# Two-operand elementwise work of the token mixers, from GpSimd to VectorE, in a hybrid RWKV-7 and HGRN2 decoder step

## The chip, the cores and the metric

One NeuronCore of a Trainium2 chip runs the whole step as one program. The metric is the device time of one execution in microseconds. The engines are named as the profile names them: PE is TensorE, DVE is VectorE, ACT is ScalarE, POOL is GpSimd, and SP starts most of the transfers. Each engine works through its own queue in order.

## What is computed

One layer of a decoder with 1024 prompt tokens and 8 sample sequences of 4 tokens each, at a model width of 1024, all in fp32:

```python
h = rmsnorm(x, norm1) * (1 + sc1) + sh1                 # sh1, sc1, gt1, ... = silu(c) @ w_ada + b_ada
p = h @ w_in                                            # 1024 -> 3840
x_rw = p_rw + (p_prev - p_rw) * mu_shift                # token shift, RWKV part (1792 columns)
y_rw = rwkv7(x_rw, state_wkv)                           # 8 heads of 64
f = lb + (1 - lb) * sigmoid(f_raw)
y_hg = hgrn2(silu(q), 1 - f, log(f), i, state_hgrn)     # 4 heads of 128
x = x + gt1 * (concat([y_rw, y_hg]) @ w_out)
h = rmsnorm(x, norm2) * (1 + sc2) + sh2
x = x + gt2 * (square(relu(h @ w_up)) @ w_down)         # 1024 -> 4096 -> 1024
y = rmsnorm(x, norm_f)
```

The new shift row and the two recurrent states, of the prompt and of each sample sequence, are returned as well.

## The kernel before

**Stages.** The profiled execution falls into two parts. The mixers (0 to 935 us) hold the first norm, the input projection, both recurrences and the conditioning vectors `mod`. From 935 us on come the output projection and the MLP, where `L1086` splits weights and `L1097` multiplies; no line of the change is run there.

**Mixers.** Tokens go in four quarters of 256; the first carries the 32 sample tokens too, 288 columns. Activations are kept transposed, features on the partitions. Before the first quarter the start computes the norm of quarter 0 (`x0` times its reciprocal root, `rstd`), the first sixteen tiles of `w_ada` (`ada_block`, subtractions at L236) and the modulation (`modulate0`, L306 to L310, and the remainder `l` at L1064). The norms of the later quarters are computed beside the projection by `norms`, whose sums of squares are added at L264.

**Projection.** A matrix product is taken in three single-pass products: every fp32 operand is split into a rounded part `hi` and a remainder `lo`. `load_w` loads a 128-column tile of `w_in` in two halves of 128x512, rounds each half on ScalarE (L172) and subtracts it from the original (L176). `gemm` then issues hi x hi, hi x lo, lo x hi (L186 to L188). The first use of each of the thirty tiles subtracts; of these sixty halves `load_in` gives three in four to GpSimd:

```python
w = self.load_w(wp, io["w_in"][m], wlo_d.get(m), m in seen, (V, V) if m in seen else [(G, G), (G, V)][self.nw % 2])
```

For tiles 14 to 29 the remainder is written to DRAM and loaded again in later quarters; for tiles 0 to 13 VectorE subtracts each time. A projected RWKV tile is evicted by ScalarE (`praw`, L583 for the samples' `psmp`), VectorE forms the shifted difference (L585, L586 for the prompt, L590, L591 for the 32 sample columns), and GpSimd does the small copies around it (L574 to L592): it fills the first column of `praw` and of `psmp` before the eviction and takes the last column into `shift_sb` after it.

**RWKV.** The prompt goes in eight groups of 128 tokens, the samples in a ninth. `rwkv_prep` loads the shifted projections of a group (`X`), forms `kk` (L687), the scaled keys (L690, L691) and the bonus term: the product at L715, a matmul, the result at L720, four transfers of it into `bot`, and the addition of a bias to `bot` at L727. After that `rwkv_attn` masks the score blocks (L758). `rwkv_inv` inverts the diagonal blocks by substitution on GpSimd (L825, L827), one short instruction after the other. `rwkv_chain` and `rwkv_finish` follow; `rwkv_finish` scales the output rows (L1014) before they are transposed. The sample group masks its operands at L954 and L994.

**HGRN.** `hgrn_mix` works head by head on a quarter. Its product at L438 is transposed by TensorE (L401). `hgrn_sample` multiplies the sample states and their operands by masks (L537, L540, L542).

**Order.** Generators are interleaved by `mixers`; the tile framework then orders each engine's queue by its own estimate of the times, so code that changes engines lets the whole order of the mixers be laid out anew. Line numbers of the profile are those of the kernel before; in the changed kernel every line from 92 on has a number smaller by one.

Of the kernel before, what the change touches and what calls it, by code (L numbers as in the profile page):

```python
# [90 lines left out]
AB = 3  # L91
XM = (0, 1, 2, 3, 4, 5, 6, 7)
EPS = 1e-6
# [39 lines left out]
class Kernel:  # L133
# [256 lines left out]
    def hgrn_mix(self, hd, qi, pool, pp, t, y_out):  # L390
# [46 lines left out]
        V.tensor_tensor(qe, q, f, op=ALU.mult)  # L437
        G.tensor_tensor(r, k, r, op=ALU.mult)  # L438
        kt = pool.tile([P, NC_, P], F32, tag="hkt", name="hkt", bufs=MB)
# [43 lines left out]
    def hgrn_sample(self, h0, pool, pp, y_out):  # L483
# [43 lines left out]
        for j in range(2):  # L527
            el = f[:, cols[j]].rearrange("p (b t) -> p b t", t=TS)[:, :, TS - 1:TS]
            po = pp.tile([SC, P], F32, tag="h", name="ps_os")
            nc.tensor.matmul(po, lhsT=att[:, j, :], rhs=vt[:, j, :], start=True, stop=False)  # L530
            for g in range(2):
                gs = slice(g * 4, (g + 1) * 4)
                s0 = pool.tile([P, 4, P], F32, tag="hs0", name="hs0", bufs=B_hs0)
                nc.sync.dma_start(s0, io["hgrn_in"][h0 + j, :, gs, :])

                qs = pool.tile([P, 4, SC], F32, tag="hqs", name="hqs", bufs=B_hqs)
                G.tensor_tensor(qs, qe[:, cols[j]].unsqueeze(1).to_broadcast([P, 4, SC]), self.tokm[:, gs, :], op=ALU.mult)  # L537
                for b in range(4):
                    nc.tensor.matmul(po, lhsT=qs[:, b, :], rhs=s0[:, b, :], start=False, stop=g == 1 and b == 3)
                G.tensor_tensor(s0, s0, el[:, gs, :].to_broadcast([P, 4, P]), op=ALU.mult)  # L540
                vm = pool.tile([SC, 4, P], F32, tag="hvm", name="hvm", bufs=B_hvm)
                G.tensor_tensor(vm, vt[:, j, :].unsqueeze(1).to_broadcast([SC, 4, P]),  # L542
                                self.seqm[0:SC, gs].unsqueeze(2).to_broadcast([SC, 4, P]), op=ALU.mult)
                pd = pp.tile([P, 4, P], F32, tag="h", name="ps_ss")
                nc.tensor.matmul(pd, lhsT=kt[:, j, :], rhs=vm, start=True, stop=True)
                V.tensor_tensor(s0, s0, pd, op=ALU.add)
                nc.scalar.dma_start(io["hgrn_s"][h0 + j, :, gs, :], s0)
                yield
            nc.scalar.activation(o[:, j, :], po, AF.Copy)
            nc.scalar.activation(sq[:, j, :], o[:, j, :], AF.Square, accum_out=ss[:, j:j + 1])  # L550
# [79 lines left out]
    def rwkv_prep(self, g, pool, pp, x_d):  # L630
# [55 lines left out]
        kk = t4("kk")  # L686
        G.tensor_tensor(kk, k, bc4(self.vec("k_k")), op=ALU.mult)  # L687
        for j in range(4):
            V.tensor_scalar(cs[:, j, :], a[:, j, :], self.vec("k_a", j), self.omka[:, j:j + 1], op0=ALU.mult, op1=ALU.add)
        G.tensor_tensor(k, k, cs, op=ALU.mult)  # L690
        G.tensor_tensor(a, a, sg, op=ALU.mult)  # L691
        sq = cs
# [21 lines left out]

        G.tensor_tensor(cs, r, k, op=ALU.mult)  # L715
        bo = kk
# [7 lines left out]
        for h in range(2):  # L724
            for e in range(2):
                nc.sync.dma_start(btq[e * 64:(e + 1) * 64, :, h, :], boq[h * 64:(h + 1) * 64, :, e, :])
        G.tensor_tensor(bt, bt, bc4(self.vec("lnx_b")), op=ALU.add)  # L727

# [212 lines left out]
    def rwkv_chain_sample(self, g, pool, pp):  # L941
# [9 lines left out]
        def alone(y):  # L951
            ax = pool.tile([P, 4, NS, 32], F32, tag="iat", name="ax", bufs=B_iat)
            for j in range(4):
                G.tensor_tensor(ax[:, j], ar[:, j, 0, y, :32].unsqueeze(1).to_broadcast([P, NS, 32]), self.tokm, op=ALU.mult)  # L954
            return ax
# [33 lines left out]
        for j in range(4):  # L989
            ps = pp.tile([P, NS, 64], F32, tag=PT[2], name="ps_Ss")  # L990
            for h in range(2):
                hs = slice(h * 64, h * 64 + 64)
                rm = pool.tile([P, NS, 64], F32, tag="U", name="rm", bufs=B_U)
                G.tensor_tensor(rm, R[:, j, h, :].unsqueeze(1).to_broadcast([P, NS, 64]),  # L994
                                self.seqm.unsqueeze(2).to_broadcast([P, NS, 64]), op=ALU.mult)
                nc.tensor.matmul(ps[hs], lhsT=bt[:, j, hs], rhs=rm, start=True, stop=True)
# [6 lines left out]
    def rwkv_finish(self, g, pool, pp, y_d):  # L1003
# [8 lines left out]
        for c in range(nch):  # L1012
            oc = g["oc"][:, c]
            G.tensor_tensor(oc, oc, rs[:, c].unsqueeze(2).to_broadcast([P, 4, 64]), op=ALU.mult)  # L1014
            for q in range(2):
# [551 lines left out]
    def mixers(self, wp, x_d, y_d):  # L1567
# [3 lines left out]
        with (tc.tile_pool(name="h", bufs=1) as hp, tc.tile_pool(name="hg", bufs=1) as hg,  # L1571
# [17 lines left out]
            def norms():  # L1589

                for qi in (1, 2, 3):
# [3 lines left out]
                    for k in range(KT):  # L1595
                        with tc.issue_after(self.last_split.ins):
                            self.square_add(hp, x(k), acc, k == 0, nc.gpsimd)
                        if k % 2:
# [21 lines left out]
            with tc.tile_pool(name="ada", bufs=1) as ap:  # L1620
# [8 lines left out]
                for k in range(KT):  # L1629
                    (nc.gpsimd if k in XM else nc.vector).tensor_tensor(x0[:, k, :], x0[:, k, :], r0, op=ALU.mult)  # L1630
                for b in range(4):
# [15 lines left out]
            def load_in(m):  # L1647
                self.nw += 1
                V, G = nc.vector, nc.gpsimd
                w = self.load_w(wp, io["w_in"][m], wlo_d.get(m), m in seen, (V, V) if m in seen else [(G, G), (G, V)][self.nw % 2])  # L1650
                seen.add(m)
                return w
# [207 lines left out]
```

## Time and profile before

| | |
|---|---|
| median of 3 runs | 1751.42 us (1748.58 to 1761.52) |
| profiled execution | 1748.32 us, span of the instructions 1746.4 us |
| granted TensorE clock, mean | 0.95 of full |
| busy, share of the span | PE 92%, DVE 73%, ACT 52%, POOL 27% |
| POOL | 466.7 us busy, 977 instructions, all before 935 us |

A busy share is a mean over stages with different limits; the table by stage divides it up. A wait is put down to the engine or transfer that came last.

### The profile page before, as it was taken

How to read it: one execution, taken by the hardware profiler on the slowest of the kernel's cores; microseconds unless marked ns; L12 is line 12 of the kernel's file. 1: busy time of each engine (PE TensorE's matmuls, PEld its weight loads, DVE VectorE, ACT ScalarE, POOL GpSimd, SP SyncE). 2: the span in 40 equal slices, each digit the busy share in tenths (PEclk: the TensorE clock that was granted, in tenths of full speed). 3: DMA queues.
4: the chain of work that ended last, by engine and by line, in shares of the span. 5: the costliest groups of instructions: out<-in, count | busy, mean ns of one | idle time of the engine just before them, and what ended most of it. 6: DMA issues, size and time to landing. Idle time of an engine off the chain costs nothing.

```text
span 1746.4 us, 38086 instructions
## 1 busy us (share of the span) xinstructions
PE 1601.1 (92%) x14224; PEld 1491.0 (85%) x14224; DVE 1277.9 (73%) x2735; ACT 903.4 (52%) x1861; POOL 466.7 (27%) x977
## 2 busy tenths in 40 slices
PE   6787998999899999899988997999999999999895
PEld 3777887787788888788867997999999999999895
DVE  7777878786655657566776669655655869798998
ACT  6446543446466665657654446455444554443351
POOL 3755738546351625436340000000000000000000
PEclk9899889999889999998988998999999999999997
DMA  7676675866677775765547533443333442324122
GB/s 261 191 226 220 200 231 155 289 211 186 180 230 219 217 227 167 220 183 156 160 143 250 202 129 116 142 140 102 105 104 111 154 147 94 111 87 139 35 75 100
DMA packets 216168, 288.66 MB, mean 165 GB/s; under 512 B 48264, under 2 KB 119304, under 8 KB 212912
## 3 DMA queue, kind: packets, MB, share of 16 engines
q1 hardware_dynamic: 198112, 263.16, 47.7%
q10 hardware_dynamic: 17776, 23.01, 3.9%
q8 instruction: 112, 1.84, 0.4%
q14 instruction: 72, 0.59, 0.1%
q0 software_dynamic: 96, 0.07, 0.0%
HBM read 225.64 MB, written 58.29 MB: 163 GB/s over the span
## 4 chain that ended last, share of the span: by engine, by line
PE 60%; DVE 17%; DMA 8%; ACT 5%; issue 4%; POOL 4%; SPq 1%; ACTq 0%; DVEq 0%; POOLq 0%
PE ps_g L1097 36%; PE ps_in L186 3%; PE ps_in L187 3%; PE ps_in L188 3%; DMA wraw<-w_in 2%; POOL itmp L825 2%; POOL ixt L827 2%; PE ps_A L755 1%; PE ps_l L429 1%; DVE acc L1384 1%; DMA x<-xT 1%; DVE wlo L1086 1%; DVE bl L1380 1%; DVE wlo L176 1%; DMA iat<-at_d 1%
## 5 line engine op out<-in xcount | busy, mean ns | idle before, releaser
L1097 PE MATMUL ps_g<-bh,whi 128*128 128x264 f32 x1792 | 370.7, 287 | 13.6 <-ACT whi L1085 8.5
L1097 PE MATMUL ps_g<-bh,wlo 128*128 128x264 f32 x1792 | 369.9, 287 | 9.0 <-DVE wlo L1086 9.0
L1097 PE MATMUL ps_g<-bl,whi 128*128 128x264 f32 x1792 | 371.0, 287 | 1.4 <-DVE bl L1380 1.4
L186 PE MATMUL ps_in<-h,whi 128*128 128x256 f32 (+1 forms) x960 | 292.2, 306 | 17.8 <-ACT psmp L583 8.4
L1097 PEld LDWEIGHTS ps_g<-bh,whi 128*128 128x128 f32 x1792 | 282.6, 190 | 14.6 <-ACT whi L1085 8.7
L1097 PEld LDWEIGHTS ps_g<-bh,wlo 128*128 128x128 f32 x1792 | 281.1, 190 | 9.7 <-DVE wlo L1086 9.7
L187 PE MATMUL ps_in<-l,whi 128*128 128x256 f32 (+1 forms) x960 | 286.7, 299 | 3.0 <-DVE l L1064 2.1
L188 PE MATMUL ps_in<-h,wlo 128*128 128x256 f32 (+1 forms) x960 | 285.7, 299 | 3.8 <-DVE wlo L176 3.7
L1097 PEld LDWEIGHTS ps_g<-bl,whi 128*128 128x128 f32 x1792 | 281.9, 190 | 1.6 <-DVE bl L1380 1.6
L186 PEld LDWEIGHTS ps_in<-h,whi 128*128 128x128 f32 x960 | 189.6, 198 | 32.2 <-ACT psmp L583 10.2
L172 ACT ACTIVATE whi<-wraw 128x512 fp32r<-128x512 f32 x240 | 147.6, 627 | 111.8 <-PE ps_in L187 55.9
L187 PEld LDWEIGHTS ps_in<-l,whi 128*128 128x128 f32 x960 | 190.2, 198 | 7.6 <-DVE l L1064 2.5
L188 PEld LDWEIGHTS ps_in<-h,wlo 128*128 128x128 f32 x960 | 189.4, 198 | 7.7 <-DVE wlo L176 4.8
L1085 ACT ACTIVATE whi<-wd 128x512 fp32r<-128x512 f32 x112 | 69.4, 630 | 163.9 <-PE ps_g L1097 127.5
L1085 ACT ACTIVATE whi<-wu 128x512 fp32r<-128x512 f32 x112 | 70.3, 632 | 145.6 <-PE ps_g L1097 140.2
L825 POOL TENSOR_TENSOR itmp<-ixt,iat 128x60 f32<-128x60 f32 (+24 forms) x248 | 92.0, 371 | 65.8 <-DMA iat<-at_d 49.4
L1086 DVE TENSOR_TENSOR wlo<-wu,whi 128x512 fp32r<-128x512 f32 x112 | 76.5, 687 | 39.3 <-ACT whi L1085 39.1
L176 DVE TENSOR_TENSOR wlo<-wraw,whi 128x512 fp32r<-128x512 f32 x99 | 77.4, 786 | 34.5 <-ACT whi L172 34.3
L827 POOL TENSOR_TENSOR ixt<-ixt,itmp 128x60 f32<-128x60 f32 (+24 forms) x248 | 90.3, 364 | 17.2
L1086 DVE TENSOR_TENSOR wlo<-wd,whi 128x512 fp32r<-128x512 f32 x112 | 76.0, 685 | 13.6 <-ACT whi L1085 13.5
L1380 DVE TENSOR_TENSOR bl<-u,bh 128x528 fp32r<-128x528 f32 x112 | 73.8, 702 | 2.3 <-ACT bh L1379 2.3
L176 POOL TENSOR_TENSOR wlo<-wraw,whi 128x512 fp32r<-128x512 f32 x45 | 60.7, 1352 | 25.8 <-ACT whi L172 19.8
(399 smaller groups left out, 3239.3 us busy)
## 6 DMA issues: line engine op xcount, KB each, us to landing
wraw<-w_in SPq DMA_DIRECT2D x240, 256.0 KB, 3.9
wlo<-wlo_d SPq DMA_DIRECT2D x96, 256.0 KB, 4.0
wu<-w_up SPq DMA_DIRECT2D x74, 256.0 KB, 2.8
u<-u_d SPq DMA_DIRECT2D x16, 1056.0 KB, 4.9
wada<-w_ada SPq DMA_DIRECT2D x64, 256.0 KB, 3.8
wd<-w_down SPq DMA_DIRECT2D x64, 256.0 KB, 2.6
u_d<-c SPq DMA_DIRECT2D x48, 264.0 KB, 3.0
wa<-w_ada SPq DMA_DIRECT2D x8, 1024.0 KB, 14.4
```

What stands on the lines that cost most here:

```text
L172: nc.scalar.activation(hi, raw, AF.Copy)
L176: eng[i].tensor_tensor(lo, raw, hi.bitcast(F32), op=ALU.subtract)
L186: nc.tensor.matmul(out, lhsT=wh, rhs=ah, start=first and k == 0, stop=False)
L187: nc.tensor.matmul(out, lhsT=wh, rhs=al, start=False, stop=False)
L188: nc.tensor.matmul(out, lhsT=wl, rhs=ah, start=False, stop=last and k == len(w) - 1)
L429: nc.tensor.matmul(ps[:, c, :], lhsT=z[:, cs], rhs=zc[:, :, 1, :], start=True, stop=True)
L825: G.tensor_tensor(tm, xt[:, 0:ns, j:j + 1].to_broadcast([P, ns, w]), at[:, j, j + 1:32].unsqueeze(1).to_broadcast([P, ns, w]), op=ALU.mult)
L827: G.tensor_tensor(dst, dst, tm, op=ALU.add)
L1085: self.nc.scalar.activation(hi, src, AF.Copy)
L1086: self.nc.vector.tensor_tensor(lo, src, hi.bitcast(F32), op=ALU.subtract)
L1097: nc.tensor.matmul(out[c], lhsT=w[x][:, k, :], rhs=a[y][:, k, c * 264:c * 264 + 264], start=first and k == 0 and j == 0, stop=last and k = ...
L1380: V.tensor_tensor(lo[:, k, :], src[:, k, :], hi[:, k, :].bitcast(F32), op=ALU.subtract)
```

## The change

These two-operand instructions of the mixers go from GpSimd to VectorE: the weight remainders of a first use (L176), `x0` times `rstd` at the start (L1630), the sums of squares of the later norms (L264), the product at L438, the masks of the sample states (L537, L540, L542, L954, L994), five of `rwkv_prep` (L687, L690, L691, L715, L727) and the scaling at L1014. The table `XM`, which named the chunks of `x0` for GpSimd, goes. GpSimd keeps the inverses (L825, L827), the small copies and fills of the projection, two subtractions of `ada_block` (L236) and the gain vectors of `modulate0`.

```diff
--- before.py
+++ after.py
@@ -89,7 +89,6 @@
 AC = 18
 HP0 = 1000
 AB = 3
-XM = (0, 1, 2, 3, 4, 5, 6, 7)
 EPS = 1e-6
 LNX_EPS = 64e-5
 DECAY0 = math.exp(-0.5)
@@ -435,7 +434,7 @@
 
         qe = pool.tile([P, 2 * P], F32, tag="hz", name="hqe", bufs=B_hz)
         V.tensor_tensor(qe, q, f, op=ALU.mult)
-        G.tensor_tensor(r, k, r, op=ALU.mult)
+        V.tensor_tensor(r, k, r, op=ALU.mult)
         kt = pool.tile([P, NC_, P], F32, tag="hkt", name="hkt", bufs=MB)
         transpose_all(r, kt)
         yield
@@ -534,12 +533,12 @@
                 nc.sync.dma_start(s0, io["hgrn_in"][h0 + j, :, gs, :])
 
                 qs = pool.tile([P, 4, SC], F32, tag="hqs", name="hqs", bufs=B_hqs)
-                G.tensor_tensor(qs, qe[:, cols[j]].unsqueeze(1).to_broadcast([P, 4, SC]), self.tokm[:, gs, :], op=ALU.mult)
+                V.tensor_tensor(qs, qe[:, cols[j]].unsqueeze(1).to_broadcast([P, 4, SC]), self.tokm[:, gs, :], op=ALU.mult)
                 for b in range(4):
                     nc.tensor.matmul(po, lhsT=qs[:, b, :], rhs=s0[:, b, :], start=False, stop=g == 1 and b == 3)
-                G.tensor_tensor(s0, s0, el[:, gs, :].to_broadcast([P, 4, P]), op=ALU.mult)
+                V.tensor_tensor(s0, s0, el[:, gs, :].to_broadcast([P, 4, P]), op=ALU.mult)
                 vm = pool.tile([SC, 4, P], F32, tag="hvm", name="hvm", bufs=B_hvm)
-                G.tensor_tensor(vm, vt[:, j, :].unsqueeze(1).to_broadcast([SC, 4, P]),
+                V.tensor_tensor(vm, vt[:, j, :].unsqueeze(1).to_broadcast([SC, 4, P]),
                                 self.seqm[0:SC, gs].unsqueeze(2).to_broadcast([SC, 4, P]), op=ALU.mult)
                 pd = pp.tile([P, 4, P], F32, tag="h", name="ps_ss")
                 nc.tensor.matmul(pd, lhsT=kt[:, j, :], rhs=vm, start=True, stop=True)
@@ -684,11 +683,11 @@
             G.tensor_copy(pt, rd[:, :, :, 63])
 
         kk = t4("kk")
-        G.tensor_tensor(kk, k, bc4(self.vec("k_k")), op=ALU.mult)
+        V.tensor_tensor(kk, k, bc4(self.vec("k_k")), op=ALU.mult)
         for j in range(4):
             V.tensor_scalar(cs[:, j, :], a[:, j, :], self.vec("k_a", j), self.omka[:, j:j + 1], op0=ALU.mult, op1=ALU.add)
-        G.tensor_tensor(k, k, cs, op=ALU.mult)
-        G.tensor_tensor(a, a, sg, op=ALU.mult)
+        V.tensor_tensor(k, k, cs, op=ALU.mult)
+        V.tensor_tensor(a, a, sg, op=ALU.mult)
         sq = cs
         S.activation(sq, kk, AF.Square)
         ps = pp.tile([8, n], F32, tag=PT[0], name="ps_ss")
@@ -712,7 +711,7 @@
             V.tensor_tensor(bk[hs, :, :, h, :], ch(k[hs]), ch(sg[hs]), op=ALU.mult)
         yield
 
-        G.tensor_tensor(cs, r, k, op=ALU.mult)
+        V.tensor_tensor(cs, r, k, op=ALU.mult)
         bo = kk
         ps = pp.tile([P, 4, n], F32, tag=PT[0], name="ps_bo")
         for j in range(4):
@@ -724,7 +723,7 @@
         for h in range(2):
             for e in range(2):
                 nc.sync.dma_start(btq[e * 64:(e + 1) * 64, :, h, :], boq[h * 64:(h + 1) * 64, :, e, :])
-        G.tensor_tensor(bt, bt, bc4(self.vec("lnx_b")), op=ALU.add)
+        V.tensor_tensor(bt, bt, bc4(self.vec("lnx_b")), op=ALU.add)
 
         g["R"] = R = [pool.tile([P, 4, 2, 64], F32, tag="R", name="R", bufs=B_R) for c in range(nch)]
         ps = pp.tile([P, nch, 4, 64], F32, tag=PT[0], name="ps_v")
@@ -951,7 +950,7 @@
         def alone(y):
             ax = pool.tile([P, 4, NS, 32], F32, tag="iat", name="ax", bufs=B_iat)
             for j in range(4):
-                G.tensor_tensor(ax[:, j], ar[:, j, 0, y, :32].unsqueeze(1).to_broadcast([P, NS, 32]), self.tokm, op=ALU.mult)
+                V.tensor_tensor(ax[:, j], ar[:, j, 0, y, :32].unsqueeze(1).to_broadcast([P, NS, 32]), self.tokm, op=ALU.mult)
             return ax
 
         ax = alone(0)
@@ -991,7 +990,7 @@
             for h in range(2):
                 hs = slice(h * 64, h * 64 + 64)
                 rm = pool.tile([P, NS, 64], F32, tag="U", name="rm", bufs=B_U)
-                G.tensor_tensor(rm, R[:, j, h, :].unsqueeze(1).to_broadcast([P, NS, 64]),
+                V.tensor_tensor(rm, R[:, j, h, :].unsqueeze(1).to_broadcast([P, NS, 64]),
                                 self.seqm.unsqueeze(2).to_broadcast([P, NS, 64]), op=ALU.mult)
                 nc.tensor.matmul(ps[hs], lhsT=bt[:, j, hs], rhs=rm, start=True, stop=True)
             V.tensor_tensor(st[:, j], ps, st[:, j], op=ALU.add)
@@ -1011,7 +1010,7 @@
         ps = pp.tile([P, nch, 2, P], F32, tag=PT[3], name="ps_oT")
         for c in range(nch):
             oc = g["oc"][:, c]
-            G.tensor_tensor(oc, oc, rs[:, c].unsqueeze(2).to_broadcast([P, 4, 64]), op=ALU.mult)
+            V.tensor_tensor(oc, oc, rs[:, c].unsqueeze(2).to_broadcast([P, 4, 64]), op=ALU.mult)
             for q in range(2):
                 nc.tensor.transpose(ps[:, c, q, :], oc[:, 2 * q:2 * q + 2, :].rearrange("p e v -> p (e v)"), self.ident)
             pv = ps[:, c].rearrange("p q (h t) -> p (q h) t", t=64)
@@ -1594,7 +1593,7 @@
                     acc = hp.tile([P, w], F32, tag="sqa", name="sqa", bufs=1)
                     for k in range(KT):
                         with tc.issue_after(self.last_split.ins):
-                            self.square_add(hp, x(k), acc, k == 0, nc.gpsimd)
+                            self.square_add(hp, x(k), acc, k == 0, nc.vector)
                         if k % 2:
                             yield
                     yield
@@ -1627,7 +1626,7 @@
                         nc.sync.dma_start(wa[b][kh], io["w_ada"][4 * b:4 * b + 4, :, kh * 4:kh * 4 + 4, :].rearrange("m p k c -> p m k c"))
                 r0 = self.rstd(hp, pg, lambda k: x0[:, k, :], w, "g")
                 for k in range(KT):
-                    (nc.gpsimd if k in XM else nc.vector).tensor_tensor(x0[:, k, :], x0[:, k, :], r0, op=ALU.mult)
+                    nc.vector.tensor_tensor(x0[:, k, :], x0[:, k, :], r0, op=ALU.mult)
                 for b in range(4):
                     self.ada_block(b, wa[b], ap, pg, ph)
                 h.append(pairs())
@@ -1646,8 +1645,8 @@
 
             def load_in(m):
                 self.nw += 1
-                V, G = nc.vector, nc.gpsimd
-                w = self.load_w(wp, io["w_in"][m], wlo_d.get(m), m in seen, (V, V) if m in seen else [(G, G), (G, V)][self.nw % 2])
+                V = nc.vector
+                w = self.load_w(wp, io["w_in"][m], wlo_d.get(m), m in seen, (V, V))
                 seen.add(m)
                 return w
```

How the queues look now, at three places. First, GpSimd in the first pass over quarter 0, about 85 us into the execution before. `praw` and `psmp` are the tiles into which the next projection is evicted. Before:

```order
L176 TENSOR_TENSOR wlo<-wraw,whi 128x512
L587 COPY shift_sb<-praw 128x1
L574 MEMSET praw 128x1
L576 COPY psmp<-shift_in 128x8
L592 COPY shift_sb<-psmp 128x8
L176 TENSOR_TENSOR wlo<-wraw,whi 128x512
L574 MEMSET praw 128x1
L576 COPY psmp<-shift_in 128x8
```

The changed kernel, the same copies (L587 is L586 now, and so on):

```order
L586 COPY shift_sb<-praw 128x1
L573 MEMSET praw 128x1
L575 COPY psmp<-shift_in 128x8
L591 COPY shift_sb<-psmp 128x8
L573 MEMSET praw 128x1
L586 COPY shift_sb<-praw 128x1
L575 COPY psmp<-shift_in 128x8
L591 COPY shift_sb<-psmp 128x8
```

The subtractions between the copies are gone from this queue.

Second, VectorE at the same place. `dsh` and `dsmp` are the shifted differences of the prompt and the samples. Before:

```order
L590 TENSOR_TENSOR dsmp<-psmp 128x32
L591 SCALAR_TENSOR_TENSOR xsh<-dsmp,vecs,psmp 128x32
L176 TENSOR_TENSOR wlo<-wraw,whi 128x512
L585 TENSOR_TENSOR dsh<-praw 128x256
L590 TENSOR_TENSOR dsmp<-psmp 128x32
L586 SCALAR_TENSOR_TENSOR xsh<-dsh,vecs,praw 128x256
L591 SCALAR_TENSOR_TENSOR xsh<-dsmp,vecs,psmp 128x32
```

The changed kernel:

```order
L175 TENSOR_TENSOR wlo<-wraw,whi 128x512
L584 TENSOR_TENSOR dsh<-praw 128x256
L175 TENSOR_TENSOR wlo<-wraw,whi 128x512
L585 SCALAR_TENSOR_TENSOR xsh<-dsh,vecs,praw 128x256
L589 TENSOR_TENSOR dsmp<-psmp 128x32
L175 TENSOR_TENSOR wlo<-wraw,whi 128x512
L590 SCALAR_TENSOR_TENSOR xsh<-dsmp,vecs,psmp 128x32
L263 TENSOR_TENSOR sqa<-sqa,sq 128x256 x2
L175 TENSOR_TENSOR wlo<-wraw,whi 128x512
```

Four subtractions of first-use weights and two additions of squares stand now between the instructions of the shift.

Third, VectorE where `rwkv_prep` hands over to the score blocks of the fourth group of the prompt, 470 us into the execution before. L720 writes `kk`, which four transfers carry into `bot`; L727 adds to `bot`. Before, with L727 in GpSimd's queue:

```order
L720 TENSOR_TENSOR kk<-X,ps_bo 128x512
L215 TENSOR_TENSOR walo<-wada,wahi 128x512
L758 TENSOR_TENSOR Aa<-ps_A,amask 128x256
L758 TENSOR_TENSOR Ar<-ps_A,amask 128x256 x2
L758 TENSOR_TENSOR Aa<-ps_A,amask 128x256
L758 TENSOR_TENSOR Ar<-ps_A,amask 128x256
L667 SCALAR_TENSOR_TENSOR cs<-cmask,sg 128x128 x4
```

The changed kernel, where L720 is L719 and L727 is L726:

```order
L719 TENSOR_TENSOR kk<-X,ps_bo 128x512
L726 TENSOR_TENSOR bot<-bot,vecs 128x512
L757 TENSOR_TENSOR Aa<-ps_A,amask 128x256
L757 TENSOR_TENSOR Ar<-ps_A,amask 128x256 x2
L686 TENSOR_TENSOR kk<-X,vecs 128x512
L757 TENSOR_TENSOR Aa<-ps_A,amask 128x256
L757 TENSOR_TENSOR Ar<-ps_A,amask 128x256
L214 TENSOR_TENSOR walo<-wada,wahi 128x512
```

The addition to `bot` stands directly behind the instruction that starts its transfers, and ahead of the mask products; a product of the next group (L687, now L686), which waits for the load of `X`, stands among these.

## Rows read from the trace of the kernel before

**Rows 1.** By stage: us; PE, PEld, DVE, ACT, POOL busy (count); PEclk, DMA, GB/s

```profile
100.00:200.00 100.00, 87.83 (x608) 80.53 (x607) 79.80 (x178) 56.78 (x140) 58.53 (x84) 0.89 0.64 205
...
300.00:400.00 100.00, 96.32 (x768) 77.09 (x762) 77.39 (x160) 44.29 (x101) 49.86 (x78) 1.00 0.78 246
...
1100.00:1200.00 100.00, 100.00 (x819) 100.00 (x819) 58.57 (x90) 49.22 (x84) 0.00 (x0) 1.00 0.38 126
```

**Rows 2.** Groups by line, GpSimd: count | busy us, mean ns | idle before

```profile
L176 POOL TENSOR_TENSOR wlo<-wraw,whi 128x512 fp32r<-128x512 f32 x45 | 60.7, 1352 | 25.8 <-ACT whi L172 19.8 <-DMA wraw<-w_in 2.6 <-PE ps_in L188 2.3
```

**Rows 3.** Timeline of VectorE: start us, us, instruction

```profile
87.87 1.29 DVE L591 SCALAR_TENSOR_TENSOR xsh<-dsmp,vecs,psmp 128x32 f32<-128x32 f32 x1
...
90.91 0.42 DVE L585 TENSOR_TENSOR dsh<-praw 128x256 f32<-128x256 f32 x1
...
92.84 0.24 DVE L591 SCALAR_TENSOR_TENSOR xsh<-dsmp,vecs,psmp 128x32 f32<-128x32 f32 x1
```

**Rows 4.** Waits of TensorE: who on whom, total us, times, longest

```profile
PE ps_in L186 <- ACT psmp L583: 8.4, 7, 3.7
```

**Rows 5.** TensorE alone, 8 us each: us, busy (matmuls), PEclk, DMA, GB/s

```profile
56.00:64.00 8.00, 8.00 (x63) 1.00 0.82 258
...
88.00:96.00 8.00, 5.79 (x39) 1.00 0.59 168
...
816.00:824.00 8.00, 8.00 (x64) 0.59 0.09 29
```

**Rows 6.** A group of VectorE beside a silent GpSimd, from the page

```profile
L1086 DVE TENSOR_TENSOR wlo<-wu,whi 128x512 fp32r<-128x512 f32 x112 | 76.5, 687 | 39.3 <-ACT whi L1085 39.1
```

**Rows 7.** VectorE alone, three stretches; the second line is L236 alone

```profile
22.30:53.60 31.30, 29.71 (x56) 0.74 0.48 168
...
22.30:53.60 31.30, 16.63 (x18) 0.74 0.48 168
...
54.00:400.00 346.00, 271.08 (x592) 0.94 0.70 218
```

**Rows 8.** Groups by line, VectorE, 54 to 200 us

```profile
L176 DVE TENSOR_TENSOR wlo<-wraw,whi 128x512 fp32r<-128x512 f32 x13 | 13.9, 1069 | 9.4 <-ACT whi L172 9.3
...
L387 DVE TENSOR_TENSOR hf<-hf 128x128 f32<-128x128 f32 x14 | 6.4, 454 | 0.2
```

**Rows 9.** GpSimd, L176 alone, 54 to 200 us

```profile
54.00:200.00 146.00, 51.42 (x38) 0.92 0.65 203
```

**Rows 10.** Timeline of VectorE at the start

```profile
15.20 4.34 DVE L236 TENSOR_TENSOR wal<-wa,wah 128x512 fp32r<-128x512 f32 x7
...
43.49 3.46 DVE L310 TENSOR_SCALAR x<-x,g_norm,mod 128x256 f32<-128x256 f32 x4
...
48.97 1.67 DVE L310 TENSOR_SCALAR x<-x,g_norm,mod 128x256 f32<-128x256 f32 x4
```

**Rows 11.** Waits of TensorE released by GpSimd, 100 to 1000 us

```profile
PE ps_tr L401 <- POOL hr L438: 6.2, 5, 2.6
...
PE ps_Os L984 <- POOL ax L954: 3.6, 1, 3.6
...
PE ps_oT L1016 <- POOL oc L1014: 2.9, 1, 2.9
```

**Rows 12.** Timeline of TensorE; in brackets the wait and its releaser

```profile
809.55 0.44 PE L401 MATMUL ps_tr<-ident,hr 128*128 128x128 f32 x2 [1.60 <-POOL hr L438]
```

**Rows 13.** Waits of GpSimd

```profile
POOL bot L727 <- DMA bot<-kk: 61.7, 8, 20.9
...
POOL kk L687 <- DMA X<-x_d: 21.0, 8, 6.0
```

**Rows 14.** Timeline of VectorE and GpSimd, fourth prompt group

```profile
469.79 0.68 DVE L720 TENSOR_TENSOR kk<-X,ps_bo 128x512 f32<-128x512 f32 x1
...
475.90 1.04 POOL L727 TENSOR_TENSOR bot<-bot,vecs 128x512 f32<-128x512 f32 x1 [7.11 <-DMA bot<-kk]
...
477.36 0.42 DVE L758 TENSOR_TENSOR Aa<-ps_A,amask 128x256 f32<-128x256 f32 x1 [5.27 <-PE ps_A L755]
```

## The prediction

> **What bounds the kernel now.** I read the page's busy shares first, then the table by stage, the groups by line, the waits, and last the timeline wherever a wait was long. By the page TensorE sets the time and GpSimd is a quarter busy (the table above); the stages say more. From 935 us on GpSimd does nothing and TensorE is full [rows 1]: the change has no line there, so those 811 us stay. All that can move lies in the mixers, 0 to 935 us. There TensorE is 88 and 96% busy in the two stages shown, VectorE near 80%, GpSimd 50 to 59% [rows 1].
>
> Two things are to be seen in the mixers. First, VectorE and GpSimd hold each other up. The same instruction, L591 over 32 columns, takes 0.24 us or 1.29 us, and the longer time is that of one GpSimd subtraction (1.35 us on average) [rows 2, 3]. Second, TensorE waits where such delays end: in the first pass a projection waits for the tile `psmp`, 8.4 us in all [rows 4], and TensorE gets through 39 matmuls in the 8 us from 88 us where an undisturbed stretch holds 63 [rows 5].
>
> **The change part by part.** It takes 192 instructions from GpSimd; the largest group is the weight remainders of L176, 45 of them, 60.7 us [rows 2]. On VectorE 109 of the 192 are of the 512-column size, which costs 0.69 us where GpSimd is silent [rows 6]; 75 have about 256 columns (0.42) [rows 3], 8 have 128 (0.42 at most): 75 + 32 + 3 = 110 us to add.
>
> Not all of that is a gain in load, since the delays go. Between 54 and 200 us six of VectorE's groups alone, from L176 (13 instructions at 1.07 us) to L387 (14 at 0.45) [rows 8], lose 25 us against their undisturbed times: 5 us in the first (13 x 0.38), 6 each in the shift instructions L586 and L591, 7 in the other three together. What enters in that stretch is 38 subtractions [rows 9], 26 us, and at most the 24 sums of squares of the three later quarters, 10 us. So VectorE's load there grows by 11 us at most, in 146 us of which a fifth is idle now [rows 1].
>
> The rows of the first `order` pair show GpSimd's queue rid of the subtractions that stood ahead of the `psmp` copies, those of the second pair the same subtractions between VectorE's shift instructions. The Trainium skill, "SBUF — State Buffer", section "Who interferes with whom", says that an instruction of VectorE with two SBUF inputs and one of GpSimd that reads SBUF exclude each other for the whole instruction; L591 and its two lengths agree. By that rule the moved instructions, which have two SBUF inputs, would in turn stop the inverses that stay. The rows bound this: each of them inside an inverse costs it one length, 0.42 to 0.69 us, and the GpSimd instruction L438 that leaves it gives about as much back. I take nothing for it.
>
> The terms, each on the path:
>
> *Start (22 to 54 us).* VectorE is busy 29.7 of 31.3 us [rows 7], so its work is the path. Eighteen subtractions take 16.6 us; before GpSimd starts, seven take 4.34, so eighteen are worth 11.2: 5.5 us lost [rows 7, 10]. Four x updates take 3.46 us beside GpSimd's subtractions and 1.67 after: 1.8 lost [rows 10]. Added: eight products at 0.42 and about three subtractions at 0.62, 5.2 us. The balance is -2; with the last copies and additions there, which run beside GpSimd as well, I take -4 (bounds -7 and 0).
>
> *First pass.* Of the 8.4 us of `psmp` waits [rows 4] I take 7 as gone: -7 (bounds -9 and 0, the latter if ScalarE or the weight loads are late next).
>
> *TensorE released by GpSimd later on.* 6.2 (L438), 3.6 (L954) and 2.9 us (L1014): 12.7 us [rows 11]. On VectorE these instructions are no longer stopped and L438 follows its producer in the same queue: -10 (bounds -13 and -3).
>
> *Clock.* After a 1.6 us wait on L438 at 809 us [rows 12] the granted clock is 0.59 of full between 816 and 824 us [rows 5], a mix of its two levels (1.2 and 2.4 GHz): 8 x 0.41 is 3.3 us of full-speed time lost in these 8 us alone. With two or three such gaps gone, but others free to appear: -4 (bounds -10 and +4).
>
> *Waits that move into VectorE's queue.* L727 waits for four transfers that L720 starts: 61.7 us on GpSimd, where it harmed nobody; L687 waits 21.0 us for its load [rows 13]. From the end of L720 to the start of L727 it is 5.4 us at 470 us [rows 14]. On VectorE one to 27 instructions stand between; the third pair shows the place with none. Behind L727 wait the mask products L758, but their own matmuls came 6.9 us after L720 there [rows 14], so most of the stall covers time in which VectorE waits anyway. I take +5 (bounds 0 and +32: six places with little cover at 5.4 us).
>
> *More load between 300 and 400 us,* where VectorE is 77% busy [rows 1] and the sample state's products arrive: +2 (bounds 0 and +10).
>
> Sum: -4 - 7 - 10 - 4 + 5 + 2 = -18 us. The profiled execution took 1748.3 us (span 1746.4); that gives 1730. It stands 3.1 us below the median shown, 1751.4, and 0.3 below the lowest of its three runs. I forecast 1730; its own range is 1714 to 1738.
>
> **The rivals.** *VectorE becomes the bound* (slower). Mechanism: between 54 and 400 us it is busy 271 of 346 us [rows 7]; with 69 us of the moved work (L176 31, L264 9, the sample state's 40 instructions 22, the preparation of three groups 7) and no relief it would be at 340, full, while the 75 us that it idles now are waits for other engines that stay. Then half of the 69 us, 35, lengthens the stretch, 12 us of releases are saved all the same, and the time is 1748 + 35 - 12 = 1771. For it: the 80% of [rows 1]; against it: the 25 us of relief. It decides once VectorE is over some 330 us busy in these 346. The Trainium skill, "Perfetto Trace Analysis", section "Optimizing Scalar/DVE Operations", advises offloading to GpSimd when VectorE is saturated, and adds that the shared port may spoil it; the trace agrees with the second half of that, by the two lengths of L591. Chance 0.11.
>
> *The waits at the head of VectorE's queue eat the gain.* If six stalls with little cover reach TensorE at 4 us each, 24 instead of 5, the sum is +1 and the time 1749; at half of that, 12 us, it is 1737; I take 1743. For it: VectorE's queue is in order, and HGRN's level products stand behind L727 in four of the groups. Against it: the mask products of [rows 14]. Chance 0.20.
>
> *TensorE is the bound anyway and the waits are replaced.* TensorE's queue holds a fixed order; where GpSimd is no longer late, ScalarE is (L401's and L476's inputs). Only the start and half of the first pass stay: -8, 1740. For it: 96% in 300 to 400 us [rows 1]. Chance 0.13. That the edits don't take effect is excluded: the rows of the three pairs show them.
>
> **How the numbers follow.** A measurement of this kernel tells about 1% (17 us) from no change. The forecast at 1730 is just beyond it, chance 0.56. The two middle rivals lie within 1% (0.33), the first is slower (0.11). The low end of the range is the sum of the good bounds on start, pass and releases with the clock's mean (-7 - 9 - 13 - 4 = -33, with +5 of costs about 1720) less some freedom, since the whole order of the mixers is laid anew: 1706. The high end takes in the middle rivals and part of the slow one: 1758.
>
> **What would show it.** Right: L591 at 0.24 us and L176 near 0.69 on VectorE in the first pass; the `psmp` waits gone; over 55 matmuls in the 8 us from 88 us; the start of the output projection earlier than 935 us by about 18 us; the stretch behind it unchanged at 811 us. Wrong: VectorE over 95% busy before 400 us, or L727 and L687 at the top of VectorE's waits with TensorE idle behind them.

## The result, and the profile after

The changed kernel takes 1766.07 us (median; 1755.25 to 1771.66) against 1750.45 us of the kernel before: a ratio of 1.0077, interval 1.0056 to 1.0097. The forecast was 1730, faster by 18; it became slower by some 14 to 16 us. The profiled execution took 1771.03 us (span 1769.3).

Much of what the prediction read in the first 300 us came out. First the page of the changed kernel, part 1 (busy us, share, instructions):

```profile
PE 1616.5 (91%) x14224; PEld 1504.5 (85%) x14224; DVE 1282.1 (72%) x2927; ACT 911.1 (51%) x1865; POOL 283.3 (16%) x785
```

GpSimd lost 183 us of work and VectorE gained 4: 192 instructions came to it, and the hold-ups that went with them were worth nearly as much. The table by stage of the changed kernel, columns as in [rows 1], and VectorE alone from 54 to 400 us (against [rows 7]):

```profile
100.00:200.00 100.00, 82.78 (x601) 75.68 (x600) 77.47 (x231) 65.08 (x153) 21.71 (x60) 0.88 0.74 233
...
300.00:400.00 100.00, 96.04 (x745) 81.35 (x745) 79.53 (x190) 49.29 (x112) 23.21 (x53) 0.95 0.76 236
```

```profile
54.00:400.00 346.00, 272.43 (x723) 0.93 0.74 230
```

VectorE has 131 instructions more in these 346 us and is busy 1.3 us longer. The single instructions show why. From the groups by line (54 to 200 us) and the timeline of VectorE in the changed kernel, where L175 was L176 and L590 was L591 [rows 3, 8]:

```profile
L175 DVE TENSOR_TENSOR wlo<-wraw,whi 128x512 fp32r<-128x512 f32 x58 | 39.7, 687 | 9.9 <-ACT whi L171 6.3 <-DMA wraw<-w_in 3.1
```

```profile
87.48 0.25 DVE L590 SCALAR_TENSOR_TENSOR xsh<-dsmp,vecs,psmp 128x32 f32<-128x32 f32 x1
...
91.89 0.24 DVE L590 SCALAR_TENSOR_TENSOR xsh<-dsmp,vecs,psmp 128x32 f32<-128x32 f32 x1
```

The subtraction went from 1.07 to 0.69 us, and the 1.29 us of L591 is gone. So is most of the wait of [rows 4], and TensorE gets through 51 matmuls from 88 to 96 us instead of the 39 of [rows 5], short of the 55 that the prediction asked for. The loss is elsewhere. TensorE alone in four stretches (us, busy, matmuls, granted clock, DMA share, GB/s), the kernel before:

```profile
54.00:300.00 246.00, 210.32 (x1677) 0.92 0.66 207
300.00:600.00 300.00, 280.30 (x2761) 0.95 0.72 219
600.00:900.00 300.00, 273.70 (x3076) 0.95 0.60 180
900.00:960.00 60.00, 52.77 (x551) 0.85 0.71 233
```

The changed kernel:

```profile
54.00:300.00 246.00, 218.26 (x1830) 0.92 0.74 227
300.00:600.00 300.00, 275.56 (x2656) 0.93 0.69 212
600.00:900.00 300.00, 276.31 (x2880) 0.89 0.57 170
900.00:960.00 60.00, 38.64 (x503) 0.75 0.44 132
```

Until 300 us it is ahead by 153 matmuls; then it gets through 105, 196 and 48 fewer. Lined up by work done (each matmul counted at the median spacing of its kind in the two traces), it is 24 us ahead at 300 us of the kernel before, 12 us at 400, 3 us at 620, and 22 us behind at 940. Two things fall: busy time near the end, and the granted clock, which is a mix of 1.2 and 2.4 GHz. Summed over these rows, length times the missing part of the clock is 59 us of full-speed time before and 89 us after; not all of it is lost, since TensorE stands idle in a part of these stretches.

Who TensorE waits for, in the changed kernel (total us, times, longest, 0 to 1000 us):

```profile
PE ps_hy L475 <- ACT ho L471: 16.6, 7, 8.2
PE ps_x L859 <- DMA XT<-xt_d: 11.0, 1, 11.0
...
PE ps_oT L1015 <- DVE oc L1013: 7.2, 1, 7.2
PE ps_ada L223 <- ACT adt L220: 6.5, 4, 3.7
PE ps_in L185 <- DVE mod L224: 4.8, 1, 4.8
...
PE ps_in L185 <- ACT psmp L582: 2.4, 3, 1.4
```

The waits on GpSimd's L438 and L954 [rows 11] are gone, and longer single ones have come, most of them on tiles that no moved instruction makes.

### The profile page after: what moved, and what is told of

It reads as the page before. It is cut to its first block, busy times and chain, and to the rows that moved or that the text cites. A ratio compares the mean times of both kernels' runs of the same rounds, so it can differ in the third digit from the quotient of the medians.

```text
span 1769.3 us, 38049 instructions
## 1 busy us (share of the span) xinstructions
PE 1616.5 (91%) x14224; PEld 1504.5 (85%) x14224; DVE 1282.1 (72%) x2927; ACT 911.1 (51%) x1865; POOL 283.3 (16%) x785
## 4 chain that ended last, share of the span: by engine, by line
PE 45%; DVE 9%; DMA 4%; ACT 2%; POOL 2%; issue 2%; SPq 0%; DVEq 0%; ACTq 0%; POOLq 0%
PE ps_g L1096 35%; DVE acc L1383 1%; DMA X<-x_d 1%; PE ps_in L185 1%; PE ps_in L186 1%; DVE wlo L1085 1%; PE ps_in L187 1%; DVE bl L1379 1%; POOL itmp L824 1%; PE ps_l L428 1%; POOL ixt L826 1%; DVE x L1122 1%; DMA wraw<-w_in 1%; DVE x L1525 1%; PE ps_A L754 1%
## 5 line engine op out<-in xcount | busy, mean ns | idle before, releaser
L171 ACT ACTIVATE whi<-wraw 128x512 fp32r<-128x512 f32 x240 | 148.1, 627 | 130.0 <-PE ps_in L186 55.2
L175 DVE TENSOR_TENSOR wlo<-wraw,whi 128x512 fp32r<-128x512 f32 x144 | 100.0, 699 | 24.4 <-ACT whi L171 20.4
L1378 ACT ACTIVATE bh<-u 128x528 fp32r<-128x528 f32 x112 | 62.8, 632 | 0.0
```

The lines of the kernel that those rows point to most:

```text
L171: nc.scalar.activation(hi, raw, AF.Copy)
L175: eng[i].tensor_tensor(lo, raw, hi.bitcast(F32), op=ALU.subtract)
L1378: A(hi[:, k, :], src[:, k, :], AF.Copy)
```

## The experiments

The trace left two theories. *A*: the waits that came along to the head of VectorE's queue (L727, L687, L954) cost the time. *B*: the planner, given other engines, laid out all queues of the mixers anew, and the new order costs the time, whoever runs the instructions. For B speaks that TensorE's queue itself stands in another order. They are told apart by holding the order. The list of instructions is the same in both kernels, in the same sequence in the code, so the order of one can be given to the other: each instruction is tied to its predecessor in the recorded queue by an edge that sets the order and adds no wait.

```diff
     with tile.TileContext(nc, schedule_with_timeline_sim=True) as tc:
         Kernel(tc, io).build()
+        hold_order(nc, tc)    # for neighbours a, b of a recorded queue:
+                              #   tc.add_manual_dep(b, a.name, NoSync)
```

The comment stands for the body of `hold_order`, which is left out here. An instruction that is on another engine than in the recorded order is left to the planner, which fits it into its new queue. The traces show that the order held: TensorE's 14224 matmuls, and ScalarE's instructions but for loads of its function tables, run in one and the same sequence before and in x1 below, and not in the changed kernel.

**x1: all 192 moved, the order of the kernel before held.**

> All 192 instructions are on VectorE, as in the changed kernel, but every instruction that was there before keeps its place in its queue (order-only edges, no waits); the moved ones are fitted into VectorE's queue. Theory A, the waits that come along to the head of VectorE's queue cost the time: still 1755 to 1775 us, with the waits on the transfers into bot and on the inverses ahead of idle TensorE. Theory B, the order of the mixers that was laid anew costs the time, not the engine: 1725 to 1740 us, since the lead of the first pass (some 20 us at 300 us) is kept to the end.

1722.58 us, ratio to before 0.9836 (0.9795 to 0.9877): far below theory A's range, and 2 us below B's. **x2: none moved, the changed kernel's order held.**

> All 192 instructions are on GpSimd as in the kernel before, but PE, ACT, SP, and all that VectorE and GpSimd share with the changed kernel stand in the order of the changed kernel. Theory A: about 1750 us or less, since the waits are back on GpSimd. Theory B: 1770 to 1795 us, the new order's loss without the first pass's gain.

1804.45 us, ratio 1.0302 (1.0261 to 1.0342). It fell outside both expectations, beyond that of B: the order alone costs more than was thought. The four corners, as ratios to the kernel before:

| | order of the kernel before | order of the changed kernel |
|---|---|---|
| on GpSimd | 1 | 1.0302 |
| on VectorE | 0.9836 | 1.0077 |

In either order the move of the engine gains: 1.6% in the old one, and 1.0077 / 1.0302, or 2.2%, in the new one. The new order costs 3.0% on GpSimd and 1.0077 / 0.9836, or 2.5%, on VectorE. Theory A is refuted and B holds: the change of engine was worth what was hoped and some more, and the order that came with it took back more than that. By the count of work done, x1 is 21 us ahead of the kernel before at 300 us, where the changed kernel was 24 ahead, and 30 us ahead at 940. The stretches of TensorE in x1 are to be set beside those above:

```profile
54.00:300.00 246.00, 222.79 (x1874) 0.95 0.72 226
300.00:600.00 300.00, 279.43 (x2763) 0.97 0.71 220
600.00:900.00 300.00, 275.77 (x3218) 0.94 0.59 180
900.00:960.00 60.00, 57.01 (x442) 0.93 0.78 266
```

The missing clock sums to 44 us, half of the changed kernel's 89. Part 1 of x1's page:

```profile
PE 1592.1 (93%) x14224; PEld 1484.2 (86%) x14224; DVE 1284.7 (75%) x2927; ACT 903.5 (53%) x1861; POOL 288.9 (17%) x785
```

The two profiled executions are 52 us apart (spans 1769.3 and 1717.1): for the same 14224 matmuls TensorE is busy 24 us longer in the changed kernel (1616.5 against 1592.1), which goes with the lower clock, and idle 28 us longer. Of x1's waits of TensorE, those that answer to the list above:

```profile
PE ps_hy L475 <- ACT ho L471: 8.4, 7, 2.3
...
PE ps_x L859 <- DMA XT<-xt_d: 3.7, 1, 3.7
PE ps_in L185 <- ACT psmp L582: 3.4, 3, 2.7
...
PE ps_oT L1015 <- DVE oc L1013: 2.9, 1, 2.9
```

Same instructions on the same engines, and half the wait.

**x3 and x4: the two halves of the move, the order of before held.** x3 moves only L176, the products of x0 (L1630) and the sums of squares (L264):

> Only the first-use weight remainders, x0 times rstd and the sums of squares go to VectorE; the order of the kernel before is held. Both theories: 1725 to 1738 us, the first pass's lead. If it is 1745 or more, the lead is lost later on because another engine or the loads set the time there.

1738.65 us, 0.994 (0.9907 to 0.9973). x4 moves the rest:

> Everything but the first-pass group moves (preparation, masks of the samples, L438, L1014); the order of the kernel before is held. Theory A: 1765 to 1785 us. Theory B: 1740 to 1752 us.

1736.61 us, 0.9938 (0.9918 to 0.9959). Both gain about 0.6%, x3 just short of what was expected and x4 a little more than B expected. The two add up to 1.2%; x1's 1.6% is somewhat more, within the intervals.

**x5 and x6: the same halves, the order left to the planner.** Two forms of B are asked here: each new order is a draw (B1), or it is bad because of what the planner sees on VectorE (B2).

> As the run with the first-pass group moved and the order held (1739 us), but the order is laid anew. Theory B1, every new order is a draw and that of the kernel before is a good one: 1750 to 1775 us. Theory B2, the new order is bad because the planner sees the preparation's and the samples' instructions on VectorE: 1735 to 1745 us, as those do not move here.

1731.37 us, 0.9876 (0.9839 to 0.9913): faster than in the order of before, which neither form expected.

> As the run with the rest moved and the order held (1737 us), but the order is laid anew. B1: 1750 to 1775 us. B2: 1765 to 1785 us, since this holds all that disturbs the planner and not the first pass's gain.

1774.46 us, 1.0117 (1.0076 to 1.0159), 38 us over x4 and within both ranges. These two alone would rather fit B2.

**x7: nothing moved, the order drawn again.**

```diff
-            nc.sync.dma_start(self.shift_in, io["shift_in"])
+            nc.scalar.dma_start(self.shift_in, io["shift_in"])
```

> The kernel before; only the load of the small tile shift_in is started by ScalarE's queue, not by SP's, which lays the order of the mixers anew with all vector work where it was. B1: 1755 to 1780 us. B2: 1744 to 1754 us.

1781.22 us, 1.0154 (1.0111 to 1.0197). No vector work moved, and 32 us are lost by the medians, 27 by the ratio. **x11** holds the order of before with the same edit, to see whether the load itself costs that:

> The kernel before with the load of shift_in started by ScalarE's queue, as in the redrawn run of 1781 us, but with the order of the kernel before held. Draw theory: 1744 to 1754 us. Rival, the load from the other queue comes late and costs the time itself: 1770 to 1785 us.

1755.73 us, 1.0032 (1.0002 to 1.0062): the load itself is worth about 0.3%, some 5 us and a little over what was expected; the order that it set off is worth the other 1.2%. x11 also comes nearest to holding the order of before with nothing else changed; the hold and the load together cost no more than that. **x10** makes this edit on the changed kernel, order free:

> The changed kernel, with the load of shift_in started by ScalarE's queue, which lays the order anew once more. Draw theory: a place of its own between 1725 and 1800 us, off the changed kernel's 1766 by more than 6. Rival, the moved instructions make the planner's order bad: 1760 to 1772 us.

1748.47 us, 0.9982 (0.9955 to 1.0009): the changed kernel in another order is no slower than before. B2 is refuted by x7 and x10 together; the moved instructions need not be there for an order to be bad, nor does it have to be bad when they are. Yet the draws are not even. Against the run that does the same work in the order of before, the new order costs 44 us in the changed kernel, 26 in x10 (its load included), 38 in x6 and 25 in x7, and only in x5 does it gain, 7 us: four of five new orders are clearly worse than that of the kernel before.

**x12: all moved, in the order that x5 was given.**

> All 192 moved, with the order held that was laid for the kernel in which the first-pass group alone moves (that one took 1731 us). The rest of the move was worth 16 us on top of the first pass in the order of before (1739 to 1723): 1712 to 1722 us. If the gain of the rest hangs on the order of before, 1726 to 1740 us.

1722.30 us, 0.9857 (0.9825 to 0.9889). A second order in which the fully moved kernel is as fast as x1. What the rest of the move brought on top of x5 is less sure: 9 us by the medians, 3 by the ratios, whose intervals overlap, and not the 16 that were expected.

**x9: x1 with the two waiting lines left on GpSimd.** L687 and L727 keep their engine; everything else is as in x1.

> All moved and the order of the kernel before held (1722.6 us), but the two lines that wait for transfers, the product at L686 and the addition at L726, stay on GpSimd. If their waits at the head of VectorE's queue reach TensorE, as the +5 us of the prediction says, 1714 to 1720 us; if they are covered, 1721 to 1727 us.

1725.14 us, 0.9871 (0.9837 to 0.9904), the same as x1 within the intervals. VectorE does stand at these lines. Its waits in the changed kernel:

```profile
DVE bot L726 <- DMA bot<-kk: 18.4, 5, 5.6
...
DVE kk L686 <- DMA X<-x_d: 14.5, 7, 3.0
```

and in x1:

```profile
DVE bot L726 <- DMA bot<-kk: 11.2, 6, 4.0
...
DVE kk L686 <- DMA X<-x_d: 7.2, 5, 2.0
```

Taking the 18 us of waiting in x1 away gains nothing that can be measured; this is net of any hold-ups that come back with the two lines on GpSimd.

**Which part of the new order costs? x8, y3 and y4** move all and hold some queues of before, with the others laid anew around them.

> The changed kernel with TensorE's queue alone in the order of the kernel before, all other queues laid anew around it. If TensorE's order is what costs: 1718 to 1730 us. If the order of ScalarE's, VectorE's or SP's queue costs: 1745 to 1766 us.

> All moved; TensorE's queue and what VectorE had before are held in the order of before, ScalarE, SP and GpSimd are laid anew. With TensorE alone held it was 1759.5 us, with all queues held 1722.6. If VectorE's order carries the difference: 1720 to 1732 us; if ScalarE's or SP's does: 1745 to 1762 us.

> All moved; TensorE, ScalarE and SP are held in the order of before, VectorE and GpSimd are laid anew. If VectorE's order carries the difference: 1745 to 1762 us; if ScalarE's or SP's does: 1720 to 1732 us. Both this and the run beside it between 1732 and 1745: the queues' orders cost together, none alone.

| queues held in the order of before | us | ratio to before |
|---|---|---|
| all (x1) | 1722.58 | 0.9836 |
| TensorE, ScalarE, SP (y4) | 1750.71 | 0.9996 (0.9963 to 1.0029) |
| TensorE (x8) | 1759.53 | 1.0058 (1.0034 to 1.0083) |
| TensorE, VectorE (y3) | 1765.01 | 1.0072 (1.0037 to 1.0107) |

To hold TensorE's order does not keep the gain, and to hold VectorE's with it does not either; y3 lies above both of its ranges. To set VectorE and GpSimd free costs 28 us; to set ScalarE, SP and GpSimd free costs 42. In each of the three tries what was laid anew around the held queues lost most of the gain. But GpSimd's queue was free in all three, and in their traces it stands in another order than in x1. A run with GpSimd alone set free is missing, so its order may carry a part of the loss in each of them; that the orders of the queues fit each other, and none carries the loss alone, is likely and not shown.

**y1 and y2: one suspected place.** The longest new wait of TensorE early on can be followed through the queues. From the timeline of the changed kernel, first SP, VectorE, then ScalarE, then TensorE (in brackets the wait and its releaser):

```profile
184.40 0.33 SPq L177 DMA_DIRECT2D wlo_d<-wlo  x1
190.73 0.30 SPq L812 DMA_DIRECT2D xt_d<-ixs  x1
191.12 0.34 SPq L168 DMA_DIRECT2D wraw<-w_in  x1
```

```profile
190.23 1.43 DVE L953 TENSOR_TENSOR ax<-ar,tokm 128x256 f32<-128x256 f32 x4 [4.05 <-POOL itmp L808]
```

```profile
194.07 0.63 ACT L171 ACTIVATE whi<-wraw 128x512 fp32r<-128x512 f32 x1 [6.52 <-DMA wraw<-w_in]
194.72 1.28 ACT L360 ACT_TABLE_LOAD   x1
...
196.44 1.28 ACT L697 ACT_TABLE_LOAD   x1
...
197.91 0.59 ACT L471 ACTIVATE ho<-ps_o,hss 128x128 f32<-128x128 f32 x2
```

```profile
198.30 0.72 PE L475 MATMUL ps_hy<-ident,ho 128*128 128x128 f32 x2 [8.20 <-ACT ho L471]
```

SP issues nothing from 184.7 to 190.7 us: it stands at L812, the transfer of an inverse's result, and the weight load L168 is behind it. ScalarE stands at the rounding of that weight (L171) with `ho` behind, and TensorE waits for `ho`. VectorE waits for the same inverse. Between the weight and `ho` ScalarE also loads a function table twice, 1.28 us each. The changed kernel's order has 58 such loads, that of the kernel before and of x1 54; the four more are 5 us of ScalarE's time. They are not the cause by themselves: x6 has 54 too, and loses 38 us. SP's waits for inverses in the changed kernel sum to 31 us:

```profile
SPq L830 <- POOL ixt L826: 25.1, 6, 10.0
...
SPq L812 <- POOL ixs L810: 5.9, 1, 5.9
```

y1 holds the changed kernel's own order and lets GpSimd start these transfers; y2 does the same in the order of before.

```diff
-            nc.sync.dma_start(xt_d[:ni], xs)
+            nc.gpsimd.dma_start(xt_d[:ni], xs)
...
-                nc.sync.dma_start(xt_d[:, sg::4, :], xt[sg * 32:(sg + 1) * 32])
+                nc.gpsimd.dma_start(xt_d[:, sg::4, :], xt[sg * 32:(sg + 1) * 32])
```

> The changed kernel with its own order held in all queues, but the transfers of the inverses' results (L812, L830) are started by GpSimd itself right behind the inverse, so that they no longer stand in SP's queue ahead of weight loads (they wait 31 us there in the changed kernel's trace, TensorE idles 8.2 us at 190 us and 11.0 us at 912 us behind two of these waits). Theory C, a good part of the new order's cost is this place in SP's queue: 1742 to 1756 us. Rival, the cost is spread over all queues: 1760 to 1768 us.

> The same edit in the order of the kernel before (all moved, 1722.6 us without it), where SP waits little for the inverses: 1719 to 1727 us by both theories; 1730 us or more if a start by GpSimd is itself dear, and then the run beside it understates what SP's waits cost.

y1: 1755.75 us, 1.0039 (1.0007 to 1.0072). y2: 1726.67 us, 0.9862 (0.9819 to 0.9904), the same as x1. y1 is 7 to 10 us faster than the changed kernel, with intervals that touch. But it did not free SP's queue. The load that fetches the result back (L845, into `XT`) is started by SP too, and SP now stands there until the transfer has landed. In the changed kernel, then in y1:

```profile
SPq L845 <- DMA xt_d<-ixt: 8.4, 10, 1.7
```

```profile
SPq L845 <- DMA xt_d<-ixt: 52.9, 9, 12.8
```

SP waits no less for the inverses in y1 than before the edit, and the two waits of TensorE that the theory named shrank and did not go:

```profile
PE ps_hy L475 <- ACT ho L471: 14.5, 7, 5.6
PE ps_x L859 <- DMA XT<-xt_d: 10.2, 1, 10.2
```

So what this place in SP's queue costs is not measured, neither by y1 nor by y2, and a run in which SP does not wait for the inverses at all is missing. The place is not the whole loss: in y4 SP waits for them no longer than in x1 (4.9 us at L830 and 3.6 at L845, against 6.4 and 5.6), and 28 us are lost. What makes up the 44 us between the changed kernel and x1 is not settled.

## Why the prediction was wrong

Where the order is held, the prediction's terms can be tested in two groups.

*Start and first pass, -4 and -7.* x3 measures them alone: 0.6%, some 9 to 10 us of the 11. The sum is right, the two terms are not, and that they make up for each other is luck. The first matmul of the projection begins at 48.1 us before and at 47.9 in x3, so the start brought next to nothing of its 4 us. By the count of work done x3 leads by 0.3 us at 54 us and by 11 at 300, so the first pass brought more than its 7, of which the `psmp` waits are 5: they went from 8.4 to 3.5 us in x3 (2.4 in the changed kernel).

*The rest: releases -10, clock -4, the queue's waits +5, load +2, together -7.* x4 measures -0.6%, about 11 us. Right in sign, and small by 4, which is within x4's interval (7 to 14 us). x4's waits, to be set against the 12.7 us of [rows 11]:

```profile
PE ps_oT L1016 <- DVE oc L1014: 2.9, 1, 2.9
PE ps_Os L984 <- DVE ax L954: 1.4, 1, 1.4
PE ps_tr L401 <- DVE hr L438: 1.2, 1, 1.2
```

They are 7 us shorter, where the prediction took 10; the wait at L1014 only changed its engine. The queue's waits were taken too high: x9 finds no gain from sending the two lines back. The clock and the load were not measured apart.

*The sum, -18.* In the order that the prediction argued from it is -25 us by the medians (x1). There the direction was right and the gain larger than forecast: the change of engine does what the prediction says, though not term by term.

*The rival that VectorE becomes the bound* is refuted: 272 us busy of 346, where 330 was its point of decision. *The rival of the waits at the head of the queue* is refuted by x1, where the two lines wait at the head of VectorE's queue and the gain is there, and by x2, where they do not and the time is longer still. *The rival of waits that are replaced* came nearest in what it looks like, ScalarE's `ho` among them, but it took TensorE's queue for a fixed order, and in the changed kernel's trace no engine's queue has kept its order.

**The step that failed** is that durations and waits of the old order were summed as if the instructions around them kept their places. The prediction knew that "the whole order of the mixers is laid anew" and used it once, as some freedom at the low end of the range. It gave it no term and no rival on the slow side, though the three order excerpts show new neighbours in GpSimd's and VectorE's queues. The term is +44 us (1722.6 to 1766.1), more than the whole sum, and its spread over orders, with the engines the same, is as large: 1722, 1723, 1748 and 1766 us for the full move, 1749, 1781 and 1804 with nothing moved. The clock term, bounded at +4, failed with it: between 54 and 960 us the missing clock rose by 30 us in the new order and fell by 15 in the old one. Also wrong by this step: the output projection begins at 955 us, not 18 us before 935; in x1 it begins at 904. The stretch behind it stayed: 814 us.

## What to carry to other kernels

Where a planner orders the queues, an edit is two changes, what it does and the order that it sets off, and the second can be the larger. Price it before predicting: make an edit that changes no work and see how far the time moves; here that was 1.5%. Where the old order is a good one, expect a new one to cost: four of five did here. And before a change is judged or dropped, run it in the old order, held by edges without waits: the change that measured 0.8% slower is 1.6% faster so, and that version (1722.6 us) beats both kernels.

## What the runs showed of the hardware that was not expected

The inverses on GpSimd take as long in the changed kernel as before, although VectorE now runs the moved instructions beside them, which have two SBUF inputs. From the page of the kernel before, then of the changed kernel (us busy, mean ns):

```profile
L825 POOL TENSOR_TENSOR itmp<-ixt,iat 128x60 f32<-128x60 f32 (+24 forms) x248 | 92.0, 371 | 65.8 <-DMA iat<-at_d 49.4
...
L827 POOL TENSOR_TENSOR ixt<-ixt,itmp 128x60 f32<-128x60 f32 (+24 forms) x248 | 90.3, 364 | 17.2
```

```profile
L824 POOL TENSOR_TENSOR itmp<-ixt,iat 128x60 f32<-128x60 f32 (+24 forms) x248 | 88.7, 358 | 116.7 <-DMA iat<-at_d 98.9
...
L826 POOL TENSOR_TENSOR ixt<-ixt,itmp 128x60 f32<-128x60 f32 (+24 forms) x248 | 91.3, 368 | 18.3
```

182 us of such work before, 180 after. This does not mean that they are not held up. In the changed kernel one and the same form takes 0.29 us with VectorE idle, and 0.63 us beside a moved instruction, which ends 0.1 us late itself (0.80 instead of 0.69 us):

```profile
492.67 0.29 POOL L824 TENSOR_TENSOR itmp<-ixt,iat 128x60 f32<-128x60 f32 x1
```

```profile
417.23 0.63 POOL L824 TENSOR_TENSOR itmp<-ixt,iat 128x60 f32<-128x60 f32 x1
```

```profile
416.89 0.80 DVE L539 TENSOR_TENSOR hs<-hs,hs_f 128x512 f32<-128x512 f32 x1
```

Over all 496 of these instructions, what each takes beyond the shortest of its form is at most 0.02 us with no VectorE instruction beside it, and 0.16 us on average beside one with two SBUF inputs. That adds up to 43 us before, 42 in the changed kernel and 50 in x1: such instructions stood beside the inverses all along, and the move adds up to 7 us of hold-up to GpSimd, for which the prediction took nothing. The other surprise is how much of the loss goes through TensorE's clock: the granted clock from 600 to 900 us is 0.89 in the changed kernel, 0.94 in x1 and 0.95 before, with TensorE's busy time within 3 us of each other (276, 276, 274).
